# Feed-forward of two superblocks by Strassen's seven products, samples moved to the first superblock

## The chip, the cores and the metric

The kernel runs on one core of one Trainium2 chip, in one launch. The metric is the time of that launch on the device in microseconds; three runs of the kernel before gave 2640.61, 2641.37 and 2642.22, median 2641.37. A core has a matrix engine (TensorE, PE in the profile; its weight loads are PEld), a vector engine (VectorE, DVE), a scalar engine (ScalarE, ACT), a general engine (GpSimd, POOL) and a queue engine that starts transfers (SyncE, SP). Matrix products land in PSUM, eight banks of 128 partitions by 512 words; all other tiles lie in SBUF.

## The reference

One layer of a decoder is computed for 2048 prompt tokens and for 8 samples of 8 tokens, which share all weights, in float32. Width 1024, hidden width 4096:

```python
q, k, v, u = _mixer_in(xp, g_mix[l], w_in[l])          # rmsnorm, then one projection of 1280 columns
attn_o = _window_attn_prompt(q, k, v, attn_sinks[l])   # 8 heads x 64, window 128, ALiBi, sinks
pool_o, pool_new = _pool_mix(u, u_prev, 0, w_pool[l], pool_scale[l])
...
x = x + jnp.concatenate([attn_o, pool_o], axis=-1) @ w_out
h = _rmsnorm(x, g_cross)                               # then cross-attention, 4 heads x 256, 256 memory tokens
x = x + o @ w_co
h = _rmsnorm(x, g_ffn)
x = x + jnp.square(jax.nn.relu(h @ w_up)) @ w_down     # the feed-forward
```

A last rmsnorm gives the output; the caches (window keys and values, pooling state, memory keys and values) are outputs too. The samples use caches of their own as input.

## The kernel before

Activations lie transposed: features on the partitions, tokens along the row. Each operand of a product is held as two tiles, a rounded one ("hi", float32r) and the rest ("lo"), and a product is three matmuls, hi by hi, hi by lo and lo by hi (`mm3` and `dense`, L108 and L267). So each evacuated result costs a copy on ScalarE and a subtraction on VectorE or POOL.

The tokens go in three **superblocks** of two halves each: 384 + 384, 384 + 384, and 256 + 320 (the last 64 of these are the samples). A prologue computes the memory's keys and values and folds them with the neighbouring weights into scratch in DRAM (`a_s`, `b_s`; L407 to L433). Then `superblock` runs for each: the input projection mixed with window attention and pooling (`mix`, L868), the output projection (L899), cross-attention (`cross`, L904; for the samples `sample_cross`, L958, mixed with it), the folded cross output (L1108), and the feed-forward. The feed-forward has 8 groups of 512 hidden columns: `up(g)` and then `down(g-1)` (L1180 to L1192), up in chunks of 24 matmuls for each half (L280 to L282), squared ReLU in `up_evac` (ScalarE L1122, POOL L1123, ScalarE L1125, VectorE L1126), down in chunks of 12 (L111 to L113), each added to the residual by VectorE (L1156).

All weights come through one `Stream` (L115): in the order in which they are used, one at a time, 512 KB by SP into an `FS` tile, rounded by ScalarE (L132) into `th`, the rest by VectorE (L133) into `tl`. `WS` has 12 such tiles, six pairs; at most five pairs stand ready ahead (`pump`, L137). During attention four of the tiles hold the keys (`kz`, L476). PSUM banks are four `MM` and four `AUX`. Work that can wait (a norm's end and its application, the next superblock's first norm) is put on the list `later` and run by `flush` (L301) a given number of chunks on. The program is written in this order; instructions of one engine are issued in one fixed order, in which an instruction that is ready early can stand ahead of its place in the text.

## Time and profile before

| what | value |
|---|---|
| median of three runs | 2641.37 us |
| profiled execution, span of its instructions | 2639.7 us (1.7 below the median) |
| granted TensorE clock, mean | 0.992 |
| busy: PE, PEld | 2565.7 us (97%), 2458.0 us (93%) |
| busy: DVE, ACT, POOL | 1302.4 (49%), 984.2 (37%), 680.7 us (26%) |
| matmuls | 15725 |
| moved by DMA | 244.76 MB, mean 93 GB/s |

A row of a group reads: line, engine, operation, what it writes and reads, its shape, how often, then total busy time, mean ns of one, and how long the engine idled before it and for whom. A matmul's own duration overlaps the next one's, so its rate is read from how many run in a stretch, not from its mean.

### The profile page before, as it was taken

To read this page: it belongs to the slowest core of one execution; us is meant where nothing else is said; L and a number is where in the kernel's file an instruction comes from. 1 tells how busy PE (TensorE), PEld (TensorE's weight loads), DVE (VectorE), ACT (ScalarE), POOL (GpSimd) and SP (SyncE) were. 2 spreads that over 40 slices of the span, in tenths; PEclk is the share of its full clock that TensorE was granted. 3 is DMA by queue.
4 is the path that set the end of the run, shared out by engine and by line. 5 is a ranking of instruction groups with operands and counts; after the bars stand their busy time and mean duration, and the time that the engine had idled before them with its cause. 6 is when DMAs were issued, how large, how long until landed. Compare 5 with 4: busy or idle time off the path is not lost. (4 is left out here: it accounts for less than half of the span.)

```text
span 2639.7 us, 39195 instructions
## 1 busy us (share of the span) xinstructions
PE 2565.7 (97%) x15725; PEld 2458.0 (93%) x15725; DVE 1302.4 (49%) x2276; ACT 984.2 (37%) x1923; POOL 680.7 (26%) x730
## 2 busy tenths in 40 slices
PE   7899999999999999999999999999999999999998
PEld 7798979999999999997999999999999669999998
DVE  7568453633333357936363333334766646334334
ACT  6666342422222244834342222223355434332231
POOL 3215322411111153433241111113334214111111
PEclk9999999999999999999999999999999999999999
DMA  7843212211111123131111111112414473222210
GB/s 261 260 130 101 72 49 74 71 64 63 61 62 64 56 72 113 45 132 56 65 58 63 65 64 64 65 56 71 140 60 149 176 266 112 87 80 81 88 57 37
DMA packets 92251, 244.76 MB, mean 93 GB/s; under 512 B 16740, under 2 KB 31524, under 8 KB 90916
## 3 DMA queue, kind: packets, MB, share of 16 engines
q1 hardware_dynamic: 92068, 242.25, 26.9%
q8 instruction: 123, 2.02, 0.3%
q14 instruction: 60, 0.49, 0.1%
HBM read 219.53 MB, written 22.69 MB: 92 GB/s over the span
## 5 line engine op out<-in xcount | busy, mean ns | idle before, releaser
L281 PE MATMUL mm<-act,w 128*128 128x384 f32 (+2 forms) x2784 | 899.1, 323 | 6.5 <-DVE act L235 5.0
L280 PE MATMUL mm<-act,w 128*128 128x384 f32 (+2 forms) x2784 | 902.8, 324 | 2.5 <-ACT act L623 1.6
L282 PE MATMUL mm<-act,w 128*128 128x384 f32 (+2 forms) x2784 | 897.4, 322 | 1.1 <-DVE w L133 0.9
L132 ACT CAST w<-f 128x1024 fp32r<-128x1024 f32 x330 | 346.9, 1052 | 737.4 <-PE mm L112 453.9
L133 DVE TENSOR_TENSOR w<-f,w 128x1024 fp32r<-128x1024 f32 x330 | 422.8, 1286 | 317.9 <-ACT w L132 312.0
L111 PE MATMUL mm<-act,w 128*128 128x384 f32 (+2 forms) x1728 | 554.1, 321 | 13.6 <-ACT act L372 8.3
L112 PE MATMUL mm<-act,w 128*128 128x384 f32 (+2 forms) x1728 | 550.3, 318 | 0.0
L113 PE MATMUL mm<-act,w 128*128 128x384 f32 (+2 forms) x1728 | 549.8, 318 | 0.0
L281 PEld LDWEIGHTS mm<-act,w 128*128 128x128 f32 x2784 | 527.3, 189 | 16.3 <-DVE act L235 6.7
L280 PEld LDWEIGHTS mm<-act,w 128*128 128x128 f32 x2784 | 527.4, 189 | 7.2 <-issue 2.3
L282 PEld LDWEIGHTS mm<-act,w 128*128 128x128 f32 x2784 | 527.3, 189 | 1.8 <-DVE w L133 1.6
L1123 POOL TENSOR_TENSOR t<-t 128x384 f32<-128x384 f32 (+2 forms) x192 | 219.0, 1141 | 1034.8 <-ACT t L1122 1034.8
L1156 DVE TENSOR_TENSOR x<-mm,x 128x384 f32<-128x384 f32 (+2 forms) x384 | 199.7, 523 | 326.5 <-PE mm L113 326.5
L111 PEld LDWEIGHTS mm<-act,w 128*128 128x128 f32 x1728 | 328.6, 190 | 15.8 <-ACT act L372 8.3
L112 PEld LDWEIGHTS mm<-act,w 128*128 128x128 f32 x1728 | 328.3, 190 | 1.2 <-DVE act L373 0.2
L113 PEld LDWEIGHTS mm<-act,w 128*128 128x128 f32 x1728 | 328.4, 190 | 0.1
L206 POOL TENSOR_TENSOR t<-t,t 128x384 f32<-128x384 f32 (+2 forms) x168 | 203.0, 1209 | 348.9 <-ACT t L205 331.4
L1126 DVE TENSOR_TENSOR act<-t,act 128x384 fp32r<-128x384 f32 (+2 forms) x192 | 103.2, 537 | 300.4 <-ACT act L1125 300.4
L1125 ACT CAST act<-t 128x384 fp32r<-128x384 f32 (+2 forms) x192 | 93.8, 488 | 237.5 <-POOL t L1123 237.5
L1122 ACT ACTIVATE t<-mm 128x384 f32<-128x384 f32 (+2 forms) x192 | 88.2, 459 | 95.2 <-PE mm L282 94.2
L205 ACT ACTIVATE t<-x 128x384 f32<-128x384 f32 (+2 forms) x140 | 68.4, 499 | 145.4 <-DVE x L1085 64.9
L111 PE MATMUL mm<-w,act 128*128 128x512 f32 x288 | 116.7, 406 | 3.2 <-ACT f L330 1.7
(184 smaller groups left out, 2199.0 us busy)
## 6 DMA issues: line engine op xcount, KB each, us to landing
f<-in_wup SPq DMA_DIRECT2D x96, 512.0 KB, 3.5
f<-in_wdn SPq DMA_DIRECT2D x96, 512.0 KB, 3.5
f<-in_win SPq DMA_DIRECT2D x30, 512.0 KB, 3.6
f<-a_s SPq DMA_DIRECT2D x24, 512.0 KB, 3.2
f<-b_s SPq DMA_DIRECT2D x24, 512.0 KB, 4.2
x<-in_x SPq DMA_DIRECT2D x6, 1536.0 KB, 7.1
f<-in_wco SPq DMA_DIRECT2D x16, 512.0 KB, 4.9
f<-in_cmk SPq DMA_DIRECT2D x16, 512.0 KB, 4.5
```

What stands on the lines that cost most here:

```text
L111: nc.tensor.matmul(ps, Wh(k), Hh(k), start=first and i == 0, stop=False)
L112: nc.tensor.matmul(ps, Wh(k), Hl(k), start=False, stop=False)
L113: nc.tensor.matmul(ps, Wl(k), Hh(k), start=False, stop=final and i == last)
L132: nc.scalar.copy(th[:], r[:, 0:1024])
L133: eng.tensor_tensor(tl[:], r[:, 0:1024], f32(th[:]), ALU.subtract)
L206: nc.gpsimd.tensor_tensor(self.acc[:, 0:n], self.acc[:, 0:n], t[:, 0:n], ALU.add)
L280: nc.tensor.matmul(ps[:, 0:n], w8(th)[:, k, :], hi(b, k), start=k == 0, stop=False)
L281: nc.tensor.matmul(ps[:, 0:n], w8(th)[:, k, :], lo(b, k), start=False, stop=False)
L282: nc.tensor.matmul(ps[:, 0:n], w8(tl)[:, k, :], hi(b, k), start=False, stop=k == 7)
L1123: nc.gpsimd.tensor_tensor(q[:, 0:n], r[:, 0:n], r[:, 0:n], ALU.mult)
L1126: nc.vector.tensor_tensor(lo, q[:, 0:n], f32(hi), ALU.subtract)
L1156: nc.vector.tensor_tensor(bl.x(m), ps[:, 0:n], bl.x(m), ALU.add)
```

## The change

**Order.** The first superblock is now 256 + 320 tokens with the samples, the other two 384 + 384. The first keeps the plain feed-forward; x is stored with the tokens of both halves side by side.

**Strassen.** In superblocks 1 and 2 the hidden product of a group is seen as a 2 x 2 by 2 x 2 block product: the two halves of the tokens by the two halves of the inner dimension, and the inner halves by the two halves of a weight group's columns. Seven products of sums (numbered 1 to 7, in the order `ORD`) take the place of eight. For up, the seven sums of the input are made once per superblock (`half_ready`), the results are combined as they come out of PSUM (`uevac`) into the hidden tiles in `FB`, where ScalarE does both ReLU and square. For down, the seven sums of the hidden are made per group (`hsplit`, POOL for the sums, two buffers `HC`), and six running sums are kept in the residual itself and in two tiles `MC` (`macc`), put together once by `merge` before the last group, whose down is plain.

**Weight sums.** Of the seven weight operands of a group two are single blocks, four are a copied block with another added to it, and one is a difference; they are made in DRAM scratch (`us_s`, `ds_s`) while superblock 0 runs: `Work.step`, called after evacuations, issues one unit each: a copy from DRAM to DRAM on ScalarE's queue, an adding transfer on POOL's, and for the one difference of a group two loads, a VectorE subtraction and a store. What is left over is issued in superblock 1. There are 113 units for 15 groups (8 of up, 7 of down) and for copies of `win`, `woa` and the last down group, and 15 differences. In superblocks 1 and 2 all weights are loaded from such scratch straight into `tl` and split in place; only superblock 0 goes through `FS`.

**Around it.** `WS` has 10 tiles instead of 12, `TS` 6 instead of 8; the keys and later `MC` share one tile of their own. Weights refill as soon as a chunk's weights are free. The cross scores run two 128-token tiles at a time, so that their weights come free one by one. A norm's closing matmul is pinned in program order.

```diff
-    [(0, 384, 0), (384, 384, 0)],
-    [(768, 384, 0), (1152, 384, 0)],
-    [(1536, 256, 0), (1792, 256, 64)],
+    [(0, 256, 0), (256, 256, 64)],
+    [(512, 384, 0), (896, 384, 0)],
+    [(1280, 384, 0), (1664, 384, 0)],
 ]
...
+ST0 = [0, 576, 1344]
+STN = [576, 768, 768]
+WIX = {3: 0, 7: 1, 2: 2, 4: 3, 5: 4, 6: 5, 1: 6}
+ORD = (2, 4, 5, 3, 1, 7, 6)
...
-def tile_hybrid_step_kernel(ctx: ExitStack, tc: tile.TileContext, io, nW=12, nF=6, nT=8):
+def tile_hybrid_step_kernel(ctx: ExitStack, tc: tile.TileContext, io, nW=10, nT=6):
...
+    us_s = drp.tile([8, 7, P, 1024], F32, name="us_s", tag="us_s")
+    ds_s = drp.tile([7, 7, P, 1024], F32, name="ds_s", tag="ds_s")
+    dn_s = drp.tile([4, P, 1024], F32, name="dn_s", tag="dn_s")
     a_s = drp.tile([2, 4, P, 1024], F32, name="a_s", tag="a_s")
...
         def emit(self):
-            key, raw, eng = self.items.popleft()
+            key, raw, eng, ext = self.items.popleft()
+            if key[0] in ("us", "ds"):
...
-            r = FS.get()
+            r = FS.get() if ext else f32(tl[:])
             w = 1024 // len(raw)
...
             for i, src in enumerate(raw):
                 nc.sync.dma_start(r[:, w * i:w * i + w], src)
-            nc.scalar.copy(th[:], r[:, 0:1024])
-            eng.tensor_tensor(tl[:], r[:, 0:1024], f32(th[:]), ALU.subtract)
-            FS.put(r)
+            i1 = nc.scalar.copy(th[:], r[:, 0:1024])
+            i2 = eng.tensor_tensor(tl[:], r[:, 0:1024], f32(th[:]), ALU.subtract)
+            self.last = (i1, i2)
+            if ext:
+                FS.put(r)
             self.ready.append((key, th, tl))
...
+                        S.add(("up", s, g, c), io["wup"][4 * g + c], ext=True)
+                for c in range(4):
+                    if g > 0:
+                        S.add(("dn", s, g - 1, c), io["wdn"][4 * (g - 1) + c], ext=True)
+            else:
+                for i in ORD:
+                    if g < 8:
+                        S.add(("us", s, g, i), us_s[g, WIX[i]])
+                for i in ORD:
+                    if 0 < g < 8:
+                        S.add(("ds", s, g - 1, i), ds_s[g - 1, WIX[i]], eng=nc.gpsimd if i in (5, 1) else None)
+                if g == 8:
+                    for c in range(4):
+                        S.add(("dn", s, 7, c), dn_s[c])
 
...
+        def split(i, src):
+            hi, lo = ACTS.get(), ACTS.get()
+            Xc[i] = (hi, lo)
+            for j in range(2):
+                c = slice(2 * nh * j, 2 * nh * j + 2 * nh)
+                nc.scalar.copy(hi[:, c], src[:, c])
+                nc.vector.tensor_tensor(lo[:, c], src[:, c], f32(hi[:, c]), ALU.subtract)
+
...
+        def half_ready(h):
+            X11, X21, X12, X22 = hx[0, 0], hx[1, 0], hx[0, 1], hx[1, 1]
+            if h == 0:
+                split(2, X11)
+                yield
+                comb(X21, X11, ALU.subtract)
+                split(4, X21)
+                yield
+            else:
+                split(5, X22)
+                yield
+                comb(X12, X22, ALU.subtract)
+                split(3, X12)
+                yield
+                comb(X11, X22, ALU.add)
+                split(1, X11)
+                yield
+                comb(X21, X11, ALU.add)
+                split(7, X21)
+                yield
+                comb(X12, X11, ALU.add)
+                split(6, X12)
+                yield
+                for j in range(2):
+                    x4 = XT[j][:, 0:4 * T].rearrange("p (a m t) -> p a m t", a=2, m=2)
+                    v = x4[:, :, 1, nh:2 * nh]
...
+        def uevac(g, i, q, ps):
+            p = ps[:, 0:nh]
+            c11, c12, c21, c22 = R(g, 0, 2 * q), R(g, 1, 2 * q), R(g, 0, 2 * q + 1), R(g, 1, 2 * q + 1)
+
+            def relu2(v):
+                nc.scalar.activation(v, v, AF.Relu)
+                nc.scalar.activation(v, v, AF.Square)
+
+            if i in (2, 5):
+                t = hold[i, q] = TS.get()
+                nc.scalar.copy(t[:, 0:nh], p)
+            if i == 4:
+                nc.vector.tensor_tensor(c21, p, hold[2, q][:, 0:nh], ALU.add)
+                hold[4, q] = ps
+                relu2(c21)
+                return
+            if i == 5:
+                p4 = hold.pop((4, q))
+                nc.vector.tensor_tensor(c11, p4[:, 0:nh], hold[5, q][:, 0:nh], ALU.add)
+                unbank(p4)
+            if i == 3:
+                t2, t5 = hold.pop((2, q)), hold.pop((5, q))
+                nc.vector.tensor_tensor(c12, p, t5[:, 0:nh], ALU.add)
+                nc.vector.tensor_tensor(c22, p, t2[:, 0:nh], ALU.add)
+                TS.put(t2, t5)
+                relu2(c12)
+            if i == 1:
+                nc.vector.tensor_tensor(c11, p, c11, ALU.subtract)
+                nc.vector.tensor_tensor(c22, p, c22, ALU.add)
+            if i == 7:
...
+                nc.vector.tensor_tensor(c11, p, c11, ALU.add)
+                relu2(c11)
+            if i == 6:
+                nc.vector.tensor_tensor(c22, p, c22, ALU.subtract)
+                relu2(c22)
+            unbank(ps)
+
+        def ups(g):
+            for i in ORD:
+                th, tl = S.next(("us", s, g, i))
+                while i not in Xc:
+                    flush()
+                Hh, Hl = Xc[i]
+                for q in range(2):
+                    ps = bank()
+                    mm3(ps[:, 0:nh], range(4), lambda k: th[:, 512 * q + P * k:512 * q + P * k + P], lambda k: tl[:, 512 * q + P * k:512 * q + P * k + P],
+                        lambda k: Hh[:, nh * k:nh * k + nh], lambda k: Hl[:, nh * k:nh * k + nh])
+                    uevac(g, i, q, ps)
+                    flush()
...
+        def hsplit(g, i, dst):
+            X11, X21, X12, X22 = R(g, 0, 0, 2), R(g, 0, 2, 2), R(g, 1, 0, 2), R(g, 1, 2, 2)
+            pre = {4: (X21, X11, ALU.subtract), 3: (X12, X22, ALU.subtract), 1: (X11, X22, ALU.add),
+                   7: (X21, X11, ALU.add), 6: (X12, X11, ALU.add)}.get(i)
+            if pre:
+                nc.gpsimd.tensor_tensor(pre[0], pre[0], pre[1], pre[2])
+            src = {2: X11, 5: X22, 4: X21, 3: X12, 1: X11, 7: X21, 6: X12}[i]
+            hi, lo = dst[:, 0:2 * nh], dst[:, 2 * nh:4 * nh]
+            nc.scalar.copy(hi, src)
+            nc.vector.tensor_tensor(lo, src, f32(hi), ALU.subtract)
+            return hi, lo
+
...
+            def make(j):
+                if j < 7:
+                    hc[j] = hsplit(g, ORD[j], HC[j % LEAD])
...
+
+            for j in range(LEAD):
+                make(j)
+            for j, i in enumerate(ORD):
+                th, tl = S.next(("ds", s, g, i))
+                Hh, Hl = hc[j]
+                for p in range(4):
+                    ps = bank()
+                    mm3(ps[:, 0:nh], range(2), lambda k: th[:, 256 * p + P * k:256 * p + P * k + P], lambda k: tl[:, 256 * p + P * k:256 * p + P * k + P],
+                        lambda k: Hh[:, nh * k:nh * k + nh], lambda k: Hl[:, nh * k:nh * k + nh])
+                    v = ps[:, 0:nh]
+                    if i == 1:
+                        nc.vector.tensor_tensor(macc(7, p), v, macc(7, p), ALU.add)
+                        nc.vector.tensor_tensor(macc(6, p), macc(6, p), v, ALU.subtract)
+                    elif g == 0 and i in (4, 5):
+                        nc.scalar.copy(macc(i, p), v)
+                    else:
+                        nc.vector.tensor_tensor(macc(i, p), v, macc(i, p), ALU.add)
+                    unbank(ps)
+                    if p % 2:
+                        flush()
+                WS.put(th, tl)
+                make(j + LEAD)
+
...
+
+            M7, M3, M2, M6 = [(lambda m, h: lambda j: role(m, h, j))(m, h) for m, h in ((0, 0), (0, 1), (1, 0), (1, 1))]
+            M4, M5 = [(lambda i: lambda j: mac(i, j))(i) for i in (4, 5)]
+            e0, e1 = (nc.gpsimd, nc.vector) if last else (nc.vector, nc.gpsimd)
+            do(nc.vector, M6, M2, ALU.subtract)
+            do(e0, M7, M4, ALU.subtract)
+            do(e0, M7, M5, ALU.subtract)
+            do(e0, M2, M4, ALU.add)
+            do(e1, M6, M3, ALU.subtract)
+            do(e1, M3, M5, ALU.add)
 
         S.resF = 0
-        up(0)
-        for g in range(1, 8):
-            up(g)
...
+            def free0():
+                FS.add(FH[0])
+                if nxt is not None:
+                    norm1(nxt[0], 7)
...
+            self.units[-1] = self.units[-1][:2] + (("in", 0),)
+            self.units += [(wo_s[4 * h:4 * h + 4, :, 0:512], io["woa"][4 * h:4 * h + 4], ("wo", 0) if h else None) for h in range(2)]
+            prev = []
+            for k, g in grp:
+                o, w = src[k]
+                cps = [(o[g, 0:2], w[g, 0:2], None), (o[g, 2:4], w[g, 2:4], None), (o[g, 4:6], w[g, 0:4:2], None)]
+                acc = [(o[g, i], w[g, b], "+" if i < 5 else (k, g)) for i, b in ((1, 3), (2, 3), (4, 1), (5, 0))]
+                for x in range(4):
+                    if x < 3:
+                        self.units.append(cps[x])
+                    if prev:
+                        self.units.append(prev[x])
+                prev = acc
+            self.units += [(dn_s[:], io["wdn"][28:32], None)]
...
+        def step(self, go=True):
+            self.n += 1
+            if self.job:
+                (k, g), at = self.job
+                t = self.tile
+                if self.n - at == DLAG:
+                    pin(nc.vector.tensor_tensor(t[:, 0:1024], t[:, 0:1024], t[:, 1024:2048], ALU.subtract))
+                elif self.n - at == DLAG + 2:
...
+            elif self.tile is not None and self.diffs:
+                k, g = self.diffs.pop(0)
+                for i in range(2):
+                    pin(nc.sync.dma_start(self.tile[:, 1024 * i:1024 * i + 1024], self.src[k][1][g, 3 * i]))
+                self.job = ((k, g), self.n)
+                return
+            if go and self.units:
+                dst, src, done = self.units.pop(0)
+                if done is None or done[0] in ("in", "wo"):
+                    pin(nc.scalar.dma_start(dst, src))
+                else:
+                    pin(nc.gpsimd.dma_start(dst, src, accum_op=ALU.add, max_dma_last_dim=8192))
```

444 lines of the change are left out of this document (321 added, 123 removed).

## The prediction

> **What bounds the kernel now.** I read the page's totals first, then the busy time by stretch, then the groups of one feed-forward stretch, and last the order of time where the feed-forward begins.
>
> ```profile
> span 2639.7 us, 39195 instructions
> PE 2565.7 (97%) x15725; PEld 2458.0 (93%) x15725; DVE 1302.4 (49%) x2276; ACT 984.2 (37%) x1923; POOL 680.7 (26%) x730
> ```
>
> Busy time by stretch (stretch, its length, then busy us and count of PE, PEld, DVE, ACT, POOL, the granted clock, the DMA share and GB/s):
>
> ```profile
> 0.00:100.00 100.00, 81.27 (x597) 78.42 (x598) 74.38 (x102) 64.12 (x112) 41.28 (x38) 0.95 0.73 253
> ...
> 600.00:700.00 100.00, 100.00 (x579) 100.00 (x578) 36.56 (x52) 22.70 (x33) 11.54 (x10) 1.00 0.19 64
> ...
> 1000.00:1100.00 100.00, 98.13 (x590) 92.89 (x589) 83.94 (x218) 60.64 (x158) 29.69 (x45) 1.00 0.21 73
> ...
> 1900.00:2000.00 100.00, 95.68 (x661) 90.24 (x660) 73.21 (x218) 61.42 (x172) 32.92 (x58) 0.95 0.28 96
> ...
> 2300.00:2400.00 100.00, 100.00 (x750) 100.00 (x749) 39.50 (x63) 27.70 (x47) 15.39 (x16) 1.00 0.25 85
> ```
>
> In the feed-forward (600 to 700) TensorE never rests, at full clock: 579 matmuls of 384 columns in 100 us, so each costs 172.7 ns there, whatever its own row says of its pipelined length. VectorE is at 37%. In the attention (1000 to 1100) VectorE is at 84% and TensorE still at 98%. So the feed-forward of the two 768-token superblocks is worth exactly its matmuls, as long as the others keep up. The profiled execution's span is 2639.7; the median of the runs is 2641.4, 1.7 more. I sum against the span and add the 1.7 at the end.
>
> **What is removed.** Per 768-token superblock, up has 8 groups x 4 chunks x 2 halves x 24 = 1536 matmuls; after it has 8 x 7 products x 2 x 12 = 1344. Down has 8 x 8 x 2 x 12 = 1536; after, groups 0 to 6 have 7 products x 4 x 6 = 168 each, and group 7 stays plain at 192: 1368. That is 360 fewer per superblock, 720 in all, still of 384 columns: 720 x 0.1727 = **124.4 us less**. The samples' move changes no count, only where the 256- and 320-token halves run.
>
> **What the other engines get, in a steady pair** (up of one group, down of the one before). TensorE: 336 x 0.1727 = 58.0 us instead of 66.3. The prices, by shape in 600 to 850 (busy us, mean ns), and the POOL adds of the whole run:
>
> ```profile
> L133 DVE TENSOR_TENSOR w<-f,w 128x1024 fp32r<-128x1024 f32 x30 | 36.8, 1226 | 40.4 <-ACT w L132 40.4
> L1156 DVE TENSOR_TENSOR x<-mm,x 128x384 f32<-128x384 f32 x64 | 35.7, 558 | 67.8 <-PE mm L113 67.8
> L132 ACT CAST w<-f 128x1024 fp32r<-128x1024 f32 x30 | 31.6, 1054 | 134.0 <-PE mm L112 106.3 <-PE mm L281 27.7
> L1126 DVE TENSOR_TENSOR act<-t,act 128x384 fp32r<-128x384 f32 x28 | 15.6, 559 | 54.3 <-ACT act L1125 54.3
> L1125 ACT CAST act<-t 128x384 fp32r<-128x384 f32 x29 | 14.9, 515 | 37.0 <-POOL t L1123 37.0
> L1122 ACT ACTIVATE t<-mm 128x384 f32<-128x384 f32 x28 | 13.7, 488 | 21.8 <-PE mm L282 21.8
> ...
> L206 POOL TENSOR_TENSOR t<-t,t 128x384 f32<-128x384 f32 x112 | 143.1, 1278 | 218.6 <-ACT t L205 202.4 <-DVE t L380 12.0 <-ACT t L202 2.0
> ...
> L206 POOL TENSOR_TENSOR t<-t,t 128x256 f32<-128x256 f32 x28 | 25.8, 923 | 52.0 <-ACT t L205 51.2
> ```
>
> Widths of 768 have no row. On a line through 384 and 1024 they cost VectorE 0.96 and ScalarE 0.84; POOL's two rows give 2.34 for 768 and 3.05 for 1024 (estimates).
> - Weights: 14 instead of 8 per pair. ScalarE 14 x 1.05 = 14.7. Two of the down weights are subtracted on POOL, so VectorE 12 x 1.226 = 14.7.
> - Up's evacuation: 16 VectorE adds = 8.9, 20 ScalarE steps = 9.8 (the square has left POOL).
> - Down's: 7 products x 4 plus 4 more for product 1 = 32 VectorE adds instead of 16: 17.9. Splitting the combined hidden: VectorE 7 x 0.96 = 6.7, ScalarE 7 x 0.84 = 5.9, POOL 5 x 2.34.
> - Sums: VectorE 48.2, ScalarE 30.4, POOL 5 x 2.34 + 2 x 3.05 = 17.8, against 58.0 of TensorE.
>
> So TensorE stays the bound on average, with VectorE at 83%. But VectorE is uneven. A product of down takes TensorE 4.14 us; VectorE owes four adds (2.23), one split (0.96) and usually one weight (1.23) = 4.42; at product 1 it owes eight adds, 6.65. A split lies in one of two buffers: it can be rewritten only when the product two before it is done, and must be there one product (4.14) later. Queued behind it on VectorE are the adds that free the PSUM banks. Product by product VectorE falls some 3.3 us behind up to product 1; the split for the last product then comes about when TensorE wants it. The up phase (8.9 + 7 weights = about 17 of 29.0) catches up.
>
> What decides is how far POOL slows VectorE. In the order of time at the start of the feed-forward (start, duration, instruction):
>
> ```profile
> 1339.59 2.21 DVE L232 SCALAR_TENSOR_TENSOR t<-x,vec,t 128x384 f32<-128x384 f32 x4
> ...
> 1346.75 1.25 POOL L235 TENSOR_TENSOR act<-t,act 128x384 fp32r<-128x384 f32 x1 [1.04 <-ACT act L233]
> 1347.05 1.36 DVE L232 SCALAR_TENSOR_TENSOR t<-x,vec,t 128x384 f32<-128x384 f32 x1
> ...
> 1349.27 3.97 DVE L133 TENSOR_TENSOR w<-f,w 128x1024 fp32r<-128x1024 f32 x2
> ...
> 1350.18 1.98 POOL L206 TENSOR_TENSOR t<-t,t 128x384 f32<-128x384 f32 x1
> ...
> 1352.12 1.81 POOL L1123 TENSOR_TENSOR t<-t 128x384 f32<-128x384 f32 x1
> ```
>
> Alone, L232 takes 0.55 (four in 2.21) and L133 1.23; beside POOL's adds they take 1.36 and 1.99, and POOL's own 1.98 instead of 1.28. The adds out of PSUM (L1156) take one operand from SBUF and keep 558. So of a pair's VectorE time the weights and splits, 21.4, are exposed. Four of the five POOL combinations wait only for the hidden to be complete, a group earlier, so they can run in the up phase, where VectorE has room; I take a stall of 1.5 us per down phase: 14 x 1.5 = **21 us more**. Ends: nothing where the slack of a product takes it all, 5 us each (70) where POOL doubles a third of the exposed time.
>
> Here the Trainium skill speaks against the change: *SBUF — State Buffer*, "Who interferes with whom", says a VectorE instruction with two SBUF inputs and a GpSimd instruction that reads SBUF exclude each other, and the second to issue waits for the whole of the first. The 1.36 above agrees with it: it ends 0.41 after POOL's row does. If every microsecond of POOL's 17.8 stopped VectorE, a pair would take 66.0, and the sum below would be 2673.
>
> **The turn into the feed-forward** (twice). Before, it costs TensorE 3.2 us of 20, with VectorE at 93%:
>
> ```profile
> 1340.00:1360.00 20.00, 16.84 (x89) 14.98 (x89) 18.63 (x26) 10.41 (x21) 12.00 (x9) 1.00 0.15 54
> ```
>
> After, between the norm of the first half (some 5 us before the last chunk of the cross output ends) and the end of the first up group, VectorE must do 16 scalings x 0.55 = 8.9, two norms of three steps at 0.56, 3.4, 14 half-splits x 0.96 = 13.4, 10 combining halves x 0.96 = 9.6, 16 evacuations 8.9, 7 weights 8.6 and the last cross evacuations 2.2: 55.0, while TensorE has 29.0 of products. All combinations are on VectorE, each product waits for its own, and only some 6 us can trail the last product. The last product then starts near 44 and ends near 48 after that chunk: 19 late, 16 more than before. Some weights will be split ahead, so I take 15 each: **30 more** (ends 12 and 44 for the two).
>
> **Smaller terms.** Merging the six sums before the last down group: 8 VectorE steps of 0.96 = 7.7 against four banks of 12 matmuls, 8.3: covered, I take 1 each; without that cover 7.7 each. The next superblock's norm starts later (inside the last two down groups): 2. Together **4** (0 to 15). The end: the last half now has 384 columns, not 256. Eight scalings after the last matmul:
>
> ```profile
> 2632.45 3.26 DVE L1173 SCALAR_TENSOR_TENSOR x<-x,vec,t 128x256 f32<-128x256 f32 x8
> ```
>
> They go to 8 x 0.55 = 4.4, and the five norm steps before grow by 128 columns on the line above, 0.13 each: **2 more**.
>
> **The transfers.** Copies: 47.2 MB of blocks (15 groups x 3 x 1.05), 9.4 of others; adding transfers 60 x 0.524 = 31.5 MB; differences 15 x 3 x 0.524 = 23.6 MB, with 15 more VectorE subtractions. By the rows above, 64 GB/s is a share of 0.19: 337 GB/s when full. One pass of 111.7 MB is then 331 us of full DMA; about 80% of the steps fall in superblock 0 from its tenth projection chunk on, near 690 us (the old last superblock, 1900 to 2639.7, less 50). Its own loads are 77 MB = 227 us. So 265 + 227 of 690: weights arrive later, yet four or five pairs are in flight, each worth 6.4 us of TensorE.
>
> ```profile
> f<-in_wup SPq DMA_DIRECT2D x96, 512.0 KB, 3.5
> ...
> f<-in_cmk SPq DMA_DIRECT2D x16, 512.0 KB, 4.5
> ```
>
> Behind each adding transfer on POOL stand superblock 0's squares, behind each copy on ScalarE its evacuations; issues cost some of that. The four weight tiles that the keys held in attention come free, but two weight tiles and two temporaries fewer remain. Grouping the cross scores in pairs, the pinned norm matmul and the earlier refill of weights change no count: nothing, covered by the same full TensorE. I take **8 more**; ends -5 (earlier loads) and, if the DMA is short, the last rival.
>
> **Sum**: 2639.7 - 124.4 + 21 + 30 + 4 + 2 + 8 = 2580.3; with 1.7, **2582**.
>
> **Rivals.**
> 1. *VectorE becomes the bound through POOL.* L133 beside POOL costs 1.65 times its own. On all 21.4 exposed that is 13.9, VectorE 62.1 per pair against 58.0: 14 x 4.1 = 57 in place of 21: **2618**. For it: the rows above. Against it: POOL is busy for only 17.8 of 58, and four of five combinations can run elsewhere.
> 2. *Nearly all is gained.* Down phases stall nothing, the turns cost 12, the rest 2: 2639.7 - 124.4 + 14 + 1.7 = **2531**. For it: TensorE at 98% under a VectorE at 84% in attention. Against it: the turn's 55 us of VectorE are counted, not guessed.
> 3. *Slower: superblock 0 runs at the pace of its transfers.* If a byte from DRAM to DRAM costs two passes and an added one three, the 111.7 MB count as 231 = 686 us, 549 of them in superblock 0; with its own 227 that is 86 over its 690. An adding transfer waits for its copy, POOL's queue waits behind it, the squares and then the PSUM banks: 2582 - 8 + 86 = **2660**. It decides from 579 us for the whole, under 193 GB/s. For it: no row shows a DRAM-to-DRAM transfer. Against it: 0.73 of the DMA already carried 253 GB/s in the first 100 us. The Trainium skill (*DMA: Bandwidth & Descriptors*, "Latency and other measured facts") gives 214 GB/s for copies between HBM tensors; by that estimate the whole is 522 us, just inside, and the sum stands; no run here shows it yet.
>
> **How the numbers follow.** Forecast 0.48 (own range 2555 to 2605), rival 1 0.20, rival 2 0.18, rival 3 0.14. The range 2535 to 2655 leaves out the far ends of 2 and 3. A measurement of this kernel tells about 0.2% (5 us) from no change. Faster: the forecast, rival 2 and most of rival 1: 0.81. Within 0.2%: the top of rival 1, 0.05. Slower: rival 3 at its price, 0.14.
>
> **What would show it.** About 15,000 matmuls, 384-column ones still 172.7 ns apart. In a Strassen stretch of 100 us VectorE near 83 and TensorE at 97 or more; below 93 is rival 1, with waits of TensorE on the down splits and longer weight rows. A hole of 15 to 19 us in TensorE at each of the two turns, waits on the combined inputs; none there is rival 2. In superblock 0, TensorE as full as before (100 in its feed-forward); waits of POOL on DMA and landing times far above 3.5 are rival 3.

## The result, and the profile after

The changed kernel takes 2851.17 us (median; 2843.09 to 2856.21) against 2641.8 for the kernel before: ratio 1.0788 (95% interval 1.077 to 1.0807), slower. The forecast was 2582, the range ended at 2655.

The page's totals of the kernel after, and its two largest queues of plain transfers (q1 is SP's, q10 ScalarE's: packets, MB, share of 16 engines):

```profile
span 2849.1 us, 39167 instructions
PE 2521.7 (89%) x15005; PEld 2372.0 (83%) x15005; DVE 1712.7 (60%) x2842; ACT 1195.4 (42%) x2195; POOL 768.6 (27%) x762
...
q1 hardware_dynamic: 121492, 313.04, 32.1%
...
q10 hardware_dynamic: 2494, 56.63, 5.3%
```

The 720 matmuls are gone (15725 to 15005), yet TensorE idles for 327 us instead of 74. ScalarE's copies come in packets of 22.7 KB on average; SP's have 2.6.

Busy time by stretch of the kernel after, columns as before:

```profile
300.00:400.00 100.00, 59.67 (x361) 53.48 (x361) 32.93 (x53) 24.17 (x47) 20.02 (x26) 0.80 0.45 134
...
340.00:360.00 20.00, 2.14 (x9) 1.15 (x7) 2.76 (x3) 1.08 (x3) 3.86 (x5) 0.60 0.51 135
360.00:380.00 20.00, 0.00 (x0) 0.00 (x0) 8.45 (x11) 6.54 (x8) 0.00 (x0) 0.50 0.19 62
...
800.00:900.00 100.00, 79.66 (x581) 78.99 (x580) 35.08 (x52) 23.27 (x43) 17.61 (x27) 0.90 0.66 204
...
1480.00:1500.00 20.00, 11.39 (x48) 10.20 (x48) 20.00 (x19) 7.04 (x11) 9.26 (x4) 0.74 0.15 52
...
1700.00:1800.00 100.00, 100.00 (x579) 100.00 (x578) 76.53 (x114) 51.13 (x72) 25.94 (x12) 1.00 0.37 127
```

Strassen's own stretch (1700 to 1800) is full, with the same 579 matmuls per 100 us. The time is lost before 1460, where no Strassen product runs: in the fronts, and in superblock 0's plain feed-forward. From 360 to 380 TensorE does nothing while the DMA is busy for 0.19 of 16 engines: no shortage of bandwidth.

Order of time there, of SP's loads and of ScalarE (start, duration, instruction; in brackets its idle time before, and what ended it):

```profile
333.91 7.36 SPq L169 DMA_DIRECT2D w<-a_s  x3
...
335.48 0.50 ACTq L1609 DMA_DIRECT2D us_s<-in_wub  x1
...
338.49 1.05 ACT L170 CAST w<-w 128x1024 fp32r<-128x1024 f32 x1 [1.39 <-DMA w<-a_s]
...
342.11 0.64 ACTq L1609 DMA_DIRECT2D us_s<-in_wub  x1
...
370.37 1.04 ACT L170 CAST w<-w 128x1024 fp32r<-128x1024 f32 x1 [26.43 <-DMA w<-a_s]
```

ScalarE stands for 26.43 us in front of one weight load, the first of the three that SP issued from 333.91. The trace says where it hung: each of the 16 DMA engines reports when its share of a load has landed, and 14 shares of this one were there by 337.0, the last two at 369.7 and 370.3. The other two loads are alike: 14 shares by 347.3, two from 371.0 on. Queued behind this wait on ScalarE is the application of the next norm (L287), which TensorE wants. The waits of the whole execution (us in total, times, longest):

```profile
ACT w L170 <- DMA w<-a_s: 115.7, 16, 26.4
...
PE mm L139 <- DVE x L1338: 49.0, 12, 19.3
...
PE mm L139 <- ACT act L287: 48.3, 2, 34.2
...
DVE mc L1593 <- DMA mc<-in_wdb: 39.7, 4, 21.0
...
DVE mc L1593 <- DMA mc<-in_wub: 23.8, 4, 9.0
```

The last two rows are a second way by which a late load costs. VectorE makes the one difference of a group (L1593) from two loaded blocks; its instructions run in a fixed order, so while it waits for the blocks, the adds to the residual (L1338) stand behind it, and TensorE waits for those.

By stage, from the last adds of cross output (L1085, L1188) and down (L1156, L1338) in each trace. "Before" has its stages put in the new order; its first front is 459.8 as the samples' old front, 324.2, plus what the first front had over the second, 472.3 - 336.7:

| stage, us | before | after | e2_small | e4_nowork | e10_late | e14_part |
|---|---|---|---|---|---|---|
| front, superblock 0 (with samples) | 459.8 | 537.6 | 489.1 | 488.7 | 472.7 | 464.4 |
| feed-forward 0, plain | 417.3 | 466.0 | 441.7 | 431.8 | 433.3 | 457.2 |
| front 1 | 336.7 | 463.2 | 340.7 | 337.1 | 336.7 | 334.2 |
| feed-forward 1, Strassen | 538.2 | 517.1 | 515.4 | 518.4 | 517.7 | 508.1 |
| front 2 | 336.7 | 346.6 | 346.8 | 346.5 | 346.5 | 345.6 |
| feed-forward 2, Strassen | 538.2 | 505.8 | 505.6 | 505.7 | 506.2 | 494.2 |

Strassen's two stages gave 54 us back; the two fronts and the plain feed-forward ahead of them cost 253. The other columns belong to the experiments.

### The profile page after: what moved, and what is told of

It is laid out like the page before. It is cut to its first block, busy times and chain, and to the rows that moved or that the text cites. A ratio compares the mean times of both kernels' runs of the same rounds, so it can differ in the third digit from the quotient of the medians.

```text
span 2849.1 us, 39167 instructions
## 1 busy us (share of the span) xinstructions
PE 2521.7 (89%) x15005; PEld 2372.0 (83%) x15005; DVE 1712.7 (60%) x2842; ACT 1195.4 (42%) x2195; POOL 768.6 (27%) x762
## 5 line engine op out<-in xcount | busy, mean ns | idle before, releaser
L334 PE MATMUL mm<-act,w 128*128 128x384 f32 (+2 forms) x1760 | 567.6, 323 | 59.8 <-DVE x L956 20.2
L139 PE MATMUL mm<-act,w 128*128 128x384 f32 (+2 forms) x1672 | 542.1, 324 | 75.1 <-DVE x L1338 49.0
L335 PE MATMUL mm<-act,w 128*128 128x384 f32 (+2 forms) x1760 | 563.8, 320 | 9.6 <-POOL act L289 5.3
L336 PE MATMUL mm<-act,w 128*128 128x384 f32 (+2 forms) x1760 | 562.0, 320 | 7.5 <-DVE w L171 7.5
L140 PE MATMUL mm<-act,w 128*128 128x384 f32 (+2 forms) x1672 | 539.7, 323 | 17.2 <-DVE act L1233 16.4
L141 PE MATMUL mm<-act,w 128*128 128x384 f32 (+2 forms) x1672 | 539.4, 323 | 0.2 <-DVE w L171 0.2
L170 ACT CAST w<-w 128x1024 fp32r<-128x1024 f32 x302 | 316.5, 1049 | 489.4 <-DMA w<-us_s 149.5
L171 DVE TENSOR_TENSOR w<-w,w 128x1024 fp32r<-128x1024 f32 x274 | 354.5, 1295 | 150.2 <-ACT w L170 148.8
L334 PEld LDWEIGHTS mm<-act,w 128*128 128x128 f32 x1760 | 340.8, 194 | 69.8 <-DVE x L956 21.6
L139 PEld LDWEIGHTS mm<-act,w 128*128 128x128 f32 x1672 | 322.6, 193 | 83.1 <-DVE x L1338 30.4
L335 PEld LDWEIGHTS mm<-act,w 128*128 128x128 f32 x1760 | 340.8, 194 | 17.0 <-POOL act L289 7.9
L336 PEld LDWEIGHTS mm<-act,w 128*128 128x128 f32 x1760 | 339.7, 193 | 14.3 <-DVE w L171 10.4
L140 PEld LDWEIGHTS mm<-act,w 128*128 128x128 f32 x1672 | 322.7, 193 | 22.9 <-DVE act L1233 19.4
L141 PEld LDWEIGHTS mm<-act,w 128*128 128x128 f32 x1672 | 322.9, 193 | 1.3 <-DVE w L171 0.4
L260 POOL TENSOR_TENSOR t<-t,t 128x384 f32<-128x384 f32 (+2 forms) x168 | 186.1, 1116 | 399.5 <-ACT t L259 393.1
L140 PE MATMUL aux<-act,w 128*128 128x384 f32 x840 | 282.5, 336 | 0.0
L139 PE MATMUL aux<-act,w 128*128 128x384 f32 x840 | 281.1, 335 | 0.0
L141 PE MATMUL aux<-act,w 128*128 128x384 f32 x840 | 281.1, 335 | 0.0
L1440 POOL TENSOR_TENSOR fb<-fb 128x768 f32<-128x768 f32 x70 | 149.8, 2142 | 381.8 <-DVE act L1444 303.9
L171 DVE TENSOR_TENSOR w<-fb,w 128x1024 fp32r<-128x1024 f32 x118 | 149.3, 1282 | 109.5 <-ACT w L170 108.3
L170 ACT CAST w<-fb 128x1024 fp32r<-128x1024 f32 x118 | 122.7, 1044 | 204.7 <-PE mm L140 152.3
L1338 DVE TENSOR_TENSOR x<-mm,x 128x320 f32<-128x320 f32 (+2 forms) x160 | 74.4, 476 | 164.0 <-PE mm L141 164.0
## 6 DMA issues: line engine op xcount, KB each, us to landing
us_s<-in_wub POOLq DMA_DIRECT2D x32, 512.0 KB, 12.4
ds_s<-in_wdb POOLq DMA_DIRECT2D x28, 512.0 KB, 13.5
```

The costliest lines, as they stand in the source:

```text
L139: nc.tensor.matmul(ps, Wh(k), Hh(k), start=first and i == 0, stop=False)
L140: nc.tensor.matmul(ps, Wh(k), Hl(k), start=False, stop=False)
L141: nc.tensor.matmul(ps, Wl(k), Hh(k), start=False, stop=final and i == last)
L170: i1 = nc.scalar.copy(th[:], r[:, 0:1024])
L171: i2 = eng.tensor_tensor(tl[:], r[:, 0:1024], f32(th[:]), ALU.subtract)
L260: nc.gpsimd.tensor_tensor(self.acc[:, 0:n], self.acc[:, 0:n], t[:, 0:n], ALU.add)
```

## The experiments

### The transfers: shape, adds, or bytes

In the built program the third copy of each group, two blocks 1 MB apart, has the block as its slowest dimension, of length 2; all copies move pieces of 64 KB. In the trace of the kernel after, exactly 15 copies report landing from only two engines, 24.4 to 30.2 us after their issue.

**e1_spread**, third copies over 16 engines in 32 KB pieces, `wo` copies partition by partition:

```
- (o[g, 4:6], w[g, 0:4:2], None)
+ (o[g, 4:6].rearrange("i (a b) c -> a i (b c)", a=16), w[g, 0:4:2].rearrange(... same ...), None)
```

> The third copy of each of the 15 groups takes two blocks that do not lie side by side; its slowest dimension is 2. Here the same bytes are copied with a slowest dimension of 16; nothing else changes. Theory A (that copy runs on two of the 16 DMA engines, and every weight load needs all 16): the load waits of 15 to 34 us in superblocks 0 and 1 go, 2851 falls by 130 us or more, to below 2720. Theory B (total bytes: rival 3 of the prediction as it was put): the bytes are the same, 2830 to 2850. Theory C (the adding transfers): 2830 to 2850.

Measured: 2731.73 us (ratio 1.0337, 1.0317 to 1.0356): 119 us back, somewhat short of what theory A asked for. The edit changes the number of engines and halves the pieces. The fixed order of instructions is all but that of the kernel after (17 of 2251 places differ on ScalarE, 26 of 2845 on VectorE), so the time was lost while the program ran, not by another program.

**e2_small**, all copies partition by partition, 4 KB pieces, 16 engines:

```
- pin(nc.scalar.dma_start(dst, src))
+ pin(nc.scalar.dma_start(dst.rearrange("i p c -> p i c"), src.rearrange("i p c -> p i c")))
```

> As the run before it, with all copies cut into 4 KB pieces with 128 as the slowest dimension instead of pieces of 32 or 64 KB. If long pieces ahead of a weight load on the same engine cost on top of theory A: 20 us or more below the run before it. If only the number of engines counts: within 10 us of it. Theories B and C: 2830 to 2850.

Measured: 2654.14 us (one run): 197 us back, the same bytes. Here the fixed order differs from the kernel after in 377 places of ScalarE, so the 78 us beyond e1_spread mix shorter pieces with another order. One of its stretches in superblock 0's feed-forward:

```profile
600.00:700.00 100.00, 100.00 (x751) 100.00 (x750) 44.15 (x67) 28.07 (x47) 19.62 (x22) 1.00 0.79 247
```

TensorE is full beside 247 GB/s.

**e3_noadds**, the adding transfers left out:

```
- pin(nc.gpsimd.dma_start(dst, src, accum_op=ALU.add, max_dma_last_dim=8192))
+ pass
```

> The 60 adding transfers are left out (so four of seven weight operands are plain blocks and the feed-forward of superblocks 1 and 2 computes something else); the copies stay as in the changed kernel. Theory A: still above 2760, since the two-engine copies stay. Theory B: the adds are 94 of 231 MB in the prediction's count, so about 40% of the loss goes: near 2750. Theory C: below 2660.

Measured: 2791.03 us (one run). The adds are worth 60 us here, as much as theory A left to them; without any of them the copies and the loads for the differences still cost 148 over the next run.

**e4_nowork**, 12 contiguous copies only:

```
+ self.units = self.units[:7] + [12 in all, none on two engines]
+ self.diffs, self.left = [], set()
```

> Only the first group's blocks, the input and output projections and the last down group are copied (12 contiguous copies, 14 MB, no adds, no differences), and all groups read these blocks, so the feed-forward of superblocks 1 and 2 computes something else with the same loads and matmuls. All theories: the whole cost of the transfers goes; by 124 less of matmul, 30 for the two turns and some 25 for the merges 2570 to 2610. If it stays above 2640, the loss is not the transfers but the smaller pools or the new order.

Measured: 2642.62 us (one run). So the transfers cost 209 as they were made and some 11 in small pieces (e2 less this; both are single runs, and other versions spread by 13 to 15 us, so the 11 gives no more than the order). The 2570 to 2610 that was expected did not come: another 69 us over the forecast without its 8 for transfers have another cause than the transfers.

### Two engines: the same copies put into the kernel before

**b1_two** and **b2_sixteen** add 15 copies of 1 MB to the kernel before, in superblock 0's feed-forward:

```
+ if s == 0 and b == 1 and c % 2 == 1 and ncp[0] < 15:
+     dst, src = c_s[i], io["wup"][2 * i:2 * i + 4:2]
+     tc.keep_in_program_order(nc.scalar.dma_start(dst, src))   # b2: both rearranged "i p c -> p i c"
```

> The kernel before, with nothing of the change but 15 added copies of two weight blocks each (1 MB, from DRAM to a DRAM buffer that nobody reads), issued from ScalarE's queue in the feed-forward of superblock 0, two per up group, one each 33 us. Their slowest dimension is the block, of length 2, as in the third copy of each group of the changed kernel. Theory A (a copy that runs on two engines holds up every weight load that needs a share of those two engines): weight splits wait 10 to 26 us behind most of them, the four or five weights in flight cover a part, 2660 to 2740. Theory B (what cost the time was the number of bytes): 15.7 MB at 300 GB/s is 52 us of transfer spread over 540 us at a DMA share of 0.19, so no change: 2637 to 2646.

> The kernel before with the same 15 added copies at the same places, but with the partition of 128 as the slowest dimension, in 4 KB pieces, so that each copy is spread over 16 engines. Theory A: the copies pass between the loads: 2638 to 2650. Theory B: the same time as with the copies on two engines.

Measured: 2643.74 (1.0014, 1.0003 to 1.0025) and 2640.35 (1.0003, 0.9993 to 1.0014). The 20 to 100 us that theory A expected on two engines did not come; there were 4. ScalarE's waits in that feed-forward of b1_two:

```profile
ACT w L134 <- DMA f<-in_wdn: 34.1, 5, 16.8
```

Before, no wait of ScalarE on a load stood among the largest there. Loads are late by up to 16.8 us, but the weights split ahead hide it, although the copies stand in pairs 17 us apart (657.48 and 674.12, say). Theory A was too short: what a late load costs depends on what stands behind it, here a stock of weights.

**b3_front** and **b4_front16** put 13 of them into the front of superblock 1:

```
+ if keys[c][0] in ("in", "wo", "B") and keys[c][1] == 1 and b == 1 and c % 2 == 1:
+     ... the same copy (b4: rearranged)
```

> The kernel before with the same two-block copies on two engines as in b1_two, 13 of them, but in the front of superblock 1 (input projection, output projection, cross output), behind every second chunk's second half, some 17 us apart where the chunks run one after the other. Theory A2: where b1_two lost 4 us behind four or five weights in flight, the front loses 5 to 10 us per copy: 2690 to 2770. If the fronts are covered as well as the feed-forward: 2640 to 2650.

> The kernel before with the same 13 copies in the same places, in 4 KB pieces over 16 engines. Theory A2: 2638 to 2655. If the bytes or the issues on ScalarE cost the time: as b3_front.

Measured: 2700.01 (1.0225, 1.0205 to 1.0246) and 2646.46 (1.0029, 1.0018 to 1.004): 60 us on two engines, 6 on sixteen, for the same bytes at the same places in the text. TensorE has three holes in that front of b3_front, of 14.4, 9.1 and 9.1 us; b4_front16 has none over 1.8. The first, from VectorE's order of time:

```profile
1177.50 1.95 DVE L891 TENSOR_TENSOR x<-mm,x 128x384 f32<-128x384 f32 x4 [19.52 <-DMA x<-in_x]
```

VectorE stands for 19.52 us in front of a load of x issued at 1156.87. Of this load 14 shares had landed by 1162.8, the last two at 1176.3 and 1177.4. It is the sign of the kernel after, made in another kernel by the copies alone. The second hole lies in the last of these stretches:

```profile
1200.00:1210.00 10.00, 10.00 (x60) 10.00 (x59) 1.67 (x3) 2.36 (x4) 2.02 (x2) 1.00 0.12 52
1210.00:1220.00 10.00, 10.00 (x59) 10.00 (x59) 1.11 (x2) 1.21 (x3) 3.04 (x3) 1.00 0.14 60
1220.00:1230.00 10.00, 10.00 (x59) 9.77 (x57) 1.34 (x3) 0.53 (x1) 1.01 (x1) 1.00 0.13 54
1230.00:1240.00 10.00, 0.93 (x3) 0.50 (x2) 9.97 (x13) 5.29 (x9) 1.90 (x1) 0.62 0.66 231
```

and the order of time on VectorE and ScalarE in it:

```profile
1230.25 4.29 DVE L135 TENSOR_TENSOR w<-f,w 128x1024 fp32r<-128x1024 f32 x3
...
1231.73 2.92 ACT L134 CAST w<-f 128x1024 fp32r<-128x1024 f32 x3
```

For 30 us the DMA is busy for 0.12 to 0.14, which is two of 16, at 52 to 60 GB/s. But the hole behind them is no late load: ScalarE waits for none between 1206 and 1231. TensorE waits for the application of a norm (L235), and the program's fixed order puts these three roundings and three subtractions ahead of it; in b4_front16 the roundings lie earlier. The shape of a copy thus changed the order of other instructions too (144 of 1939 places on ScalarE differ). How much of the 54 us between the two is late loads and how much is order stays open.

### Two engines or long pieces

**e8_two**: e2_small with the third copy of each group alone put back on two engines in 64 KB pieces. **e16_two4k**: that copy still on two engines, in 4 KB pieces.

```
- nc.scalar.dma_start(dst.rearrange("i p c -> p i c"), src.rearrange("i p c -> p i c"))
+ nc.scalar.dma_start(dst, src)                           # e8_two, third copies only
+ nc.scalar.dma_start(dst, src, max_dma_last_dim=4096)    # e16_two4k, third copies only
```

> The changed kernel with all copies in small pieces over 16 engines (2654 in one run), but with the third copy of each group alone put back as it was, its two blocks outermost, on two engines. 53 copies as before, 15 of them changed. Theory A2 (a two-engine copy holds up the weight loads issued behind it by up to 30 us, which costs time where few weights are in flight or where several such copies come close together): 80 to 120 of the 197 us come back, 2735 to 2775. Theory C (the size of the pieces of all copies was what counted): 2655 to 2675.

> As e8_two (2832: small pieces everywhere but in the third copy of each group, which has its two blocks outermost and runs on two engines in 64 KB pieces), with the third copy still on two engines but in 4 KB pieces. Theory N (the number of engines alone: a megabyte through two engines occupies them for 19 us, however it is cut): 2800 to 2840, as e8_two. Theory L (the length of the pieces: on these two engines each small piece of a weight load waits behind a whole 64 KB piece of the copy): 2655 to 2700, near e2_small's 2654.

Measured: 2832.44 (1.0727, 1.0667 to 1.0787; two runs) and 2751.88 (1.0424, 1.0381 to 1.0468). Fifteen of 53 copies bring back 178 of the 197 us, more than either theory of e8_two expected, and e16_two4k lies between its two. Between e8_two and e16_two4k, whose fixed orders agree but for 12 places of ScalarE and none of VectorE, lie 80 us: those are the length of the pieces. The 98 of e16_two4k over e2_small are two engines and another order together (258 places of ScalarE differ). e8_two, waits of the whole execution:

```profile
ACT w L170 <- DMA w<-a_s: 119.1, 16, 24.9
```

e2_small, the same view:

```profile
ACT w L170 <- DMA w<-a_s: 44.6, 14, 9.5
```

and e16_two4k, the same view:

```profile
ACT w L170 <- DMA w<-a_s: 40.0, 14, 9.9
```

With 4 KB pieces the loads of `a_s` wait no longer than in e2_small, with 64 KB pieces almost three times as long. The records of the DMA engines show why. In the kernel after, from 351 to 363, the two engines that carry a copy take turns between three queues: a load's packet of 4 KB for 0.16 us, the copy's of 64 KB for 2.42, an adding transfer's of 8 KB for 0.63. So the load comes forward by one packet on each of them every 3.2 us. In e16_two4k the copy's packets take 0.16 us too, and the load's come every 0.31 us. An estimate from these: an engine's share of a 512 KB load is 8 packets of 4 KB, and 8 turns of 3.2 us are 26 us, as long as ScalarE's wait.

What the 4 KB pieces on two engines cost has another sign. e16_two4k, ScalarE's order of time:

```profile
257.13 7.13 ACTq L1612 DMA_DIRECT2D ds_s<-in_wdb  x1
...
299.41 13.73 ACTq L1612 DMA_DIRECT2D us_s<-in_wub  x1
313.24 0.47 ACT L259 ACTIVATE t<-x 128x320 f32<-128x320 f32 x1 [13.44 <-issue]
...
337.20 0.47 ACT L259 ACTIVATE t<-x 128x320 f32<-128x320 f32 x1 [22.23 <-DMA ds_s<-in_wdb]
```

Four issues of copies hold ScalarE's queue for 5.5 to 13.7 us, 39 in all, each 4 to 15 us behind the issue of a two-engine copy; in no other version does an issue take over 2 us. What stands behind them on ScalarE, the work for a norm among it, comes that much later. The trace has the landing of these two-engine copies at 35.5 us in the median. The adding transfers into their blocks wait for that in POOL's queue, and with them the squares of the norm that TensorE waits for, though that is the smaller part. e16_two4k, waits from 200 to 1420:

```profile
PE aux L268 <- POOL t L260: 29.1, 4, 13.1
```

and the same row of e2_small:

```profile
PE aux L268 <- POOL t L260: 15.6, 4, 4.7
```

How the 98 us divide among these and the other order was not followed, and no run took one of them alone.

The Trainium skill has the rule: in *DMA: Bandwidth & Descriptors*, "Rules for kernel authors", an outermost dimension under 16 confines a transfer to that many engines, and the 128 partitions should stand there. The traces agree, with two engines reporting for each such copy, and so do the runs, with 54 us between b3_front and b4_front16 and 98 between e16_two4k and e2_small, order included. "Queues, rings and completion order" of the same page says that an engine serves its queues in turn, a whole packet at a time; the three queues' turns in the kernel after agree with that.

### What Strassen's stages lose

**e6_unpin**: e2_small with the norm's closing matmul not pinned.

```
- pin(nc.tensor.matmul(pm[:, 0:n], ones[:], self.acc[:, 0:n], start=True, stop=True))
+ nc.tensor.matmul(pm[:, 0:n], ones[:], self.acc[:, 0:n], start=True, stop=True)
```

> The changed kernel with all copies in small pieces over 16 engines (2654 in one run), and with the norm's closing matmul free to move in the program's order instead of pinned where it is emitted. If the pinned matmul is what TensorE waits 7 us for at the norms of superblock 0 and of the samples: 2635 to 2648. If those waits only stand in place of others behind them: 2650 to 2656.

Measured: 2665.66 (1.0084, 1.0055 to 1.0113), 12 us over e2_small's one run. The matmul's wait on POOL's sums grows from 17.6 to 39.3 us in all: left free it seems to stand ahead of its sums in TensorE's order. Both theories were wrong: neither allowed for a loss of this size.

The merge is read from the order of time of e4_nowork:

```profile
1721.11 2.64 DVE L1490 TENSOR_TENSOR x<-x 128x768 f32<-128x768 f32 x2
...
1723.68 12.53 DVE L1490 TENSOR_TENSOR x<-x,mc 128x768 f32<-128x768 f32 x6
...
1727.93 4.99 POOL L1490 TENSOR_TENSOR x<-x 128x768 f32<-128x768 f32 x2
...
1732.88 4.99 POOL L1490 TENSOR_TENSOR x<-x,mc 128x768 f32<-128x768 f32 x2
...
1736.13 2.82 DVE L171 TENSOR_TENSOR w<-w,w 128x1024 fp32r<-128x1024 f32 x1
```

and its stretch:

```profile
1720.00:1740.00 20.00, 6.04 (x34) 5.75 (x33) 20.00 (x15) 4.39 (x9) 19.68 (x11) 0.72 0.01 2
```

Beside POOL six of the eight VectorE steps take 2.09 us instead of the 0.96 estimated (the other two 1.32), and the weight 2.82 instead of 1.23. The eight last 15.1, and TensorE loses 14.

**e7_lazy**: e2_small with two subtractions in front, and the other merge terms on VectorE in halves just before the adds they belong to.

```
- do(e0, M7, M4, ALU.subtract) ... do(e1, M3, M5, ALU.add)
+ do(nc.vector, M6, M2, ALU.subtract); do(nc.vector, M6, M3, ALU.subtract)
+ # in down(7), before each add: the 384-wide terms of that half
```

> The changed kernel with all copies in small pieces over 16 engines, and with the merge of the six sums taken apart: in front of the last down group VectorE does only two subtractions, the four other terms are added on VectorE in halves of 384 just before the adds of the last group that they belong to, and POOL does none of it. Theory: the merge's cost comes from VectorE's steps running at 2.1 to 2.5 us beside POOL's (13.9 and 7.0 us of TensorE's waits in the two merges): 2633 to 2642. Rival: VectorE is short in the last down group either way, so the waits move into it: 2649 to 2657.

Measured: 2647.95 (1.0027, 1.0014 to 1.0041), 6 below e2_small's one run: between theory and rival. The merge's wait fell from 14 to 10.

**e9_tail**: e7_lazy with the last four chunks of the cross output half by half.

```
- add_evac2, after=after_co))
+ add_evac2, tail=4 if s else 3, after=after_co))
```

> The changed kernel with small pieces and the merge taken apart (2648), and with the last four chunks of the cross output of the two 768-token superblocks ordered half by half instead of the last three, so that the first half's norm and its two combinations can run one chunk earlier. Theory: the turn's hole of 15 us is VectorE's work that comes too late, so 4 us more of TensorE's work in front of it shorten it by 4 at each turn: 2636 to 2645. If the second half's chain alone sets the hole: 2646 to 2651.

Measured: 2633.55 (0.9975, 0.9962 to 0.9988), somewhat beyond what was expected: the first version that beats the kernel before. By the stages of the two profiles, 21 us apart, Strassen's parts gained 3 and 2 over e7_lazy and the fronts of superblocks 1 and 2, where the tail is, 7 and 2; another 7 lie in superblock 0, which the edit doesn't touch. The runs of both spread by 13 to 15 us, so parts of this size are not told apart from the spread.

### Superblock 0

**e10_late** (e4_nowork) and **e11_late** (e9_tail) issue nothing in the front of superblock 0; e11_late then issues at every step of its feed-forward. **e14_part** (e9_tail) leaves out only the steps of the two projections, and issues at five of nine.

```
- work.step(s > 0 or len(qdone) > 9)     + work.step(s > 0)
- work.step(c < 6)                       + work.step(s > 0 and c < 6)
- work.step(0 < gi < len(groups) - 1)    + work.step(s > 0 and ...)     # e10, e11 only; L1190 likewise
- work.step(work.n % 2 == 0)             + work.step(True)              # e11; e14: work.n % 9 in (0, 2, 4, 6, 8)
```

> The kernel with only 12 contiguous copies and no adds or differences (e4_nowork, 2643), its copies held back until the feed-forward of superblock 0, so that the front of superblock 0 has none; as there, Strassen's weights are not the true sums. In e4_nowork that front took 488.7 us where the old first front plus the samples' old front would give 459.8. Theory P (the front is longer because the samples now meet the first superblock's preparation of the weights, and because fewer tiles are left): it stays within 3 us of 488.7. Theory Q (the copies on ScalarE's queue and their traffic lengthen it): it falls by 10 to 29 us, and the whole to 2614 to 2635.

> The version with small pieces, the merge taken apart and the longer tail (2633.5), with the transfers held back in the same way: none in the front of superblock 0, and one at every step of its feed-forward instead of every second. Theory P: 2630 to 2640. Theory Q: 2608 to 2625.

> The version with small pieces, the merge taken apart and the longer tail (2633.5), with no transfer at the steps of the input and output projection of superblock 0 (those of its cross attention and cross output stay), and a transfer at five of nine steps of its feed-forward instead of one of two. If the copies in the projections cost 16 us, and the feed-forward of superblock 0 bears five of nine as it bears one of two: 2615 to 2625. If what is saved in the front is lost in the feed-forward, which lost 100 us at one per step: 2628 to 2650.

Measured: e10_late 2625.41 (0.9939, 0.9915 to 0.9963), its first front 16 us shorter than e4_nowork's. Theory Q holds, for 16 of the 29. One stretch of e4_nowork:

```profile
200.00:300.00 100.00, 84.35 (x504) 74.32 (x504) 58.08 (x173) 50.46 (x144) 38.07 (x74) 0.85 0.53 178
```

and the same of e10_late, with TensorE 11 us busier and the DMA share down by 0.23:

```profile
200.00:300.00 100.00, 95.71 (x678) 91.39 (x677) 63.01 (x169) 56.14 (x150) 49.76 (x81) 0.97 0.30 96
```

e11_late: 2699.04 (1.022, 1.0201 to 1.0239), outside both theories; what the front gained, the feed-forward lost many times over:

```profile
500.00:600.00 100.00, 79.56 (x585) 79.13 (x584) 33.52 (x49) 24.63 (x46) 19.58 (x25) 0.90 0.96 316
600.00:700.00 100.00, 77.60 (x556) 77.08 (x555) 35.68 (x55) 19.59 (x31) 17.48 (x21) 0.88 0.94 294
```

Here the DMA is nearly full, at 294 to 316 GB/s, and TensorE waits. The way is again over the differences: VectorE waits for their blocks,

```profile
DVE mc L1591 <- DMA mc<-in_wdb: 68.6, 5, 23.2
```

and TensorE, behind it, for VectorE's adds (L1341), 88 us in the whole execution against 10 in e14_part. e14_part, in between: 2623.27 (0.9935, 0.9919 to 0.9952), 18 us under the kernel before and the best full version. Its DMA is nearly full, but TensorE too:

```profile
500.00:600.00 100.00, 99.33 (x743) 99.10 (x742) 44.44 (x66) 30.26 (x52) 24.19 (x27) 1.00 0.92 279
```

## Why the prediction was wrong

**The step that failed is the transfers' term.** It priced 111.7 MB at 337 GB/s, as if each transfer could use the whole DMA, and took 8 us. It measured 209, and the shares of the loads show where: two of 16 land up to 33 us behind the other 14, because two engines carry a copy in packets of 64 KB. Per stage it knew only sums of bytes, and never asked how one copy is laid out: two blocks outermost, so two engines. In small pieces over all engines the same bytes cost some 11 over the 12 copies left in e4_nowork, and those cost 17 in the front (e4_nowork less e10_late). By these, of which e2_small and e4_nowork are single runs, the term with the copies laid out well would have been 11 to 28 us: the forecast's 8 was then too low but not far off.

**Rival 3** named the place, superblock 0 and what follows it, and the signs, late weights and waits of POOL, but not the mechanism: its price was a DMA short of bandwidth, and it decided from under 193 GB/s. e2_small moves the bytes beside a full TensorE at 247 GB/s, while the kernel after loses time in the stretches shown, where the DMA's share is 0.19 to 0.66. A DMA nearly full while TensorE waits is seen in e11_late. The 214 GB/s of the Trainium skill (*DMA: Bandwidth & Descriptors*, "Latency and other measured facts"), which it was weighed against, is exceeded by these rates, which count the loads too; no run here shows DRAM to DRAM alone.

**Point by point**, in e4_nowork, where the transfers are out of the way (2640.8 of span against 2572 of the forecast without them):

| term | forecast | measured, and from what |
|---|---|---|
| matmuls | -124.4 | 720 fewer at 579 per 100 us: as predicted |
| stalls in down | +21 | about 0: TensorE 99.6 to 100 in its stretches |
| the two turns | +30 | 24: 16.1 and 14.2 idle, less 3.2 each |
| merge, boundary, tail | +6 | 32: 14 and 7 at the merges, 9 behind the first (in front 2), 1.5 at the end |
| superblock 0 | 0 | 43 by the stages |
| clock after holes, small waits | none | some 24, what is left of the two Strassen stages; 8 of it shown as clock |

The clock after a hole is seen in two stretches of e4_nowork behind the first merge:

```profile
1739.60:1742.40 2.80, 2.80 (x9) 2.80 (x10) 1.21 (x3) 1.43 (x3) 2.56 (x4) 0.50 0.00 0
1742.40:1745.20 2.80, 2.80 (x18) 2.80 (x17) 0.56 (x1) 1.20 (x3) 2.64 (x3) 0.99 0.00 0
```

TensorE is busy in both, with nine matmuls at a granted clock of 0.50 and then eighteen at 0.99. In the two Strassen stages 56 matmuls run at 0.32 us instead of 0.173 while the clock's record is 0.50, which is 8 us; the other 16 were not followed.

The stall in down fell away because VectorE, at 76 to 83 of 100 in these stretches, has the room that was counted, and its instructions seldom meet one of POOL: the weights (L171) cost 1.30 on average, not 1.65 times 1.23. Rival 1 falls with that, not because the rule of *SBUF — State Buffer*, "Who interferes with whom", in the Trainium skill that spoke for it fails. Single instructions do wait, in the steady stretches too; e4_nowork from 1300 to 1700 (shortest, median and longest in ns):

```profile
L1444 DVE TENSOR_TENSOR act<-fb,act x46: 943/954/2690, 1319.3 to 1699.1; 128x768 fp32r<-128x768 f32 x46
```

The turn was right in size and cause, VectorE at 20.00 of 20. The merge was wrong: it was priced at VectorE's own pace, though the plan gave POOL work at the same moment. The row for L133 beside POOL, on which the stalls in down were argued, was not applied there.

Superblock 0 was not costed at all, since the samples' move changes no matmul. Of its 43 us some 14 to 16 are copies in the front. The other 27 or so stay open: it has fewer weight and temporary tiles than the same work had in the last place, and the samples now meet the preparation of the weights; no run told these apart. The signs listed for rival 3 did show (two-engine copies landing after 24.4 to 30.2 us, adding transfers after 12.4 to 13.5 in the median instead of the 7.6 to 8.0 of e2_small, holes in superblock 0), so the list pointed at the right place, with the wrong reason.

## What to carry to other kernels

Price a transfer by its layout before its bytes: put the 128 partitions outermost and keep the pieces short, or one background copy on a few engines makes every load behind it late, while the DMA looks idle. A late load costs where nothing is in stock behind it, so the same copies can be nearly free in one stage (4 us for 15) and cost some 5 to 12 us each in others, the changed order of instructions included; a test in the well-stocked stage alone would have shown next to nothing. When two layouts of a copy are compared, compare the order of the other instructions too: here it changed with the layout. And when a plan puts VectorE and POOL to work at one moment, take both at the pace they have side by side.

## What was not expected of the hardware

A copy of 1 MB on two engines in 64 KB pieces ran at 52 to 60 GB/s and landed after 27.0 us in the median (the kernel after); over 16 engines in 4 KB pieces the copies of e2_small took 6.0. Two shares of a load of 512 KB landed 33 us behind the other 14, and ScalarE stood 26.43 us for them. On two engines, 64 KB pieces instead of 4 KB were worth 80 us for 15 copies, yet behind copies of 4 KB pieces the issue of the next copy held ScalarE's queue for 5.5 to 13.7 us. With plain and adding transfers mixed, the DMA was busy for 0.94 to 0.96 at 294 to 316 GB/s with TensorE starved; at 279 (0.92) TensorE was still full. After a hole of 14 us the granted clock was still 0.50 for 2.8 us of full work, so a hole costs more than its length.
